# State-space layer of a decoder trunk: projections reordered and placed by tables, decay differences moved from VectorE to ScalarE, output product in two passes

## The chip, the cores and the metric

The kernel runs on one core of a Trainium2 chip. The metric is the device time of one execution in microseconds (us). Five engines matter. TensorE (PE) does the matrix products and ScalarE (ACT) the activations. VectorE (DVE) and GpSimd (POOL) do elementwise work, and SyncE (SP) issues the transfers (DMA).

## The reference

512 tokens of width 1024 go through two layers, each followed by a gated MLP with a short convolution, and a final normalisation. The first layer mixes by pooling and windowed attention; the second is the state-space layer that the change rewrites:

```python
def ssd_mixer(h, w_in, conv_w, conv_b, dt_bias, A_log, D_skip, norm_w, w_out):
    proj = h @ w_in
    z, xbc, dt = jnp.split(proj, [SSM_D_INNER, SSM_D_INNER + SSM_CONV_DIM], axis=-1)
    xbc = jax.nn.silu(causal_dwconv(xbc, conv_w, conv_b))
    xs, Bm, Cm = jnp.split(xbc, ...)
    dt = jax.nn.softplus(dt + dt_bias)
    A = -jnp.exp(A_log)
    y = ssd_scan(xs, dt, A, Bm, Cm) + D_skip[:, None] * xs
    y = y.reshape(B, S, SSM_D_INNER) * jax.nn.silu(z)
    y = rms_norm(y, norm_w, SSM_NORM_EPS)
    return y @ w_out

# in ssd_scan, by chunks of 128 tokens, with a = dt * A and its running sum a_cs in a chunk:
    Lmat = jnp.exp(jnp.where(tril, a_cs[..., :, None] - a_cs[..., None, :], -jnp.inf))
    CB = jnp.einsum("bclgn,bcsgn->bgcls", Cc, Bc)
    y_diag = jnp.einsum("bgcls,bgrcls,bcsgrp->bclgrp", CB, Lmat, X)
    states = jnp.einsum("bclgn,bgrcl,bclgrp->bcgrpn", Bc, decay, X)
    # state of chunk c+1 = state of chunk c * chunk_decay + states[c]
    y_off = jnp.einsum("bclgn,cbgrpn,bgrcl->bclgrp", Cc, prev, jnp.exp(a_cs))
    return y_diag + y_off
```

There are 8 groups of 4 heads with 64 features each, a state of 128, and 4 chunks.

## The kernel before

Everything lies with features on the 128 partitions and the 512 tokens along the free axis. A product of the trunk is a weight tile of eight 128x128 blocks against eight activation tiles. Weights and activations are split in a high and a low part, so each block costs three matmuls of 128x512 (L151 high by high, L152 high by the activation's low part, L153 the weight's low part): 24 matmuls for a product. `load_split` brings a weight tile: a DMA into `w`, ACT makes the high part `wh` (L143), DVE the low part `wl` (L144); each has three buffers.

The program is mixer, MLP, `ssm`, MLP. In the mixer the order of PE is written out by hand; `ssm` and the MLPs lie outside that block, and there a scheduler orders the instructions of every engine, with the place in the program as the priority. Whatever order comes out, each engine then works through its own list strictly in order.

In `ssm` the step sizes and decays come first (L663 to L665 are the running sums; L672 writes them to the scratch tensor `scr`). Then each group does six products: gates z (two), x (two), B and C. x, B and C go through a convolution (L286, L290, L292) and a Silu (L698 for z, L690 for the others). B and x are transposed (L710, L719), and B against C gives `cb` (L728, L730). For each of four chunks a DMA spreads four rows of `scr` over the partitions into `R` (L740). Then:

```python
for r in range(4):
    V.tensor_scalar(L[:, r, :], R[:, r, :], acs[:, h0 + r : h0 + r + 1], 0.0,
                    op0=ALU.subtract, op1=ALU.min)          # L743, DVE
A.activation(L[:], L[:], AF.Exp)                            # L745
```

L746 multiplies by `cb`, L749 and L750 make the state's factor (ACT, POOL). L754 and L757 are the output matmuls into `yp`, L760 the state product (from `XD`, which POOL makes in L723), and L763 or L766 the state update. L772 and L774 add the skip term and the gate into `yv`, and `stat.add` gathers squares (L224 ACT, L225 POOL).

After the eight groups `split_scaled` splits the 16 tiles `yv` (L204 on ACT for the high part, L205 on DVE for the low part), and eight output products of 48 matmuls with `wso` follow, one after the other.

The helpers `Line` (a list of product steps with side work placed at numbered steps) and `ahead` (issues a weight load one product early) are there before, used by the mixer.

## Time and profile before

| | us |
|---|---|
| median of the runs | 1314.21 |
| the other two runs | 1313.87 and 7378.31 |
| the profiled execution | 1316.71 |
| its span in the trace | 1314.9 |

The mean granted clock of TensorE is 0.992 in the profiled execution. Between 510 us (the feature steps of `ssm`, L628) and 943 us (the sums of the second MLP, L232) lies the part that the change rewrites. An engine's busy time is the sum of its instructions; rows of a timeline give the start, the length and, in brackets, the idle time just before and what ended it.

### The profile page before, as it was taken

The numbers are of one execution on the slowest core, as the hardware profiler recorded it, in microseconds if no ns is written. First come the engines' busy times: TensorE is split into PE (matmuls) and PEld (weight loads), VectorE is DVE, ScalarE is ACT, GpSimd is POOL, SyncE is SP. The second block draws the span as 40 slices with busy tenths as digits, with TensorE's granted clock in tenths as the row PEclk, the third lists the DMA queues.
The fourth block names the chain that finished last, engine by engine and source line by source line (L and its number), as shares of the span: only waits on it lengthen the run. The fifth ranks groups of instructions, "written<-read, shape, count | busy, mean of one in ns | idle before, by whom it ended". The sixth has DMA issues, their size and how long they took to land.

```text
span 1314.9 us, 16324 instructions
## 1 busy us (share of the span) xinstructions
PE 1288.2 (98%) x6280; PEld 1055.2 (80%) x6280; DVE 868.6 (66%) x1342; ACT 596.5 (45%) x829; POOL 182.4 (14%) x168
## 2 busy tenths in 40 slices
PE   8999999999999999999999999899999999999997
PEld 5766888888888887888888888688888888888887
DVE  7664577467547763788888888864587467547753
ACT  6254554234324443665556655633354234334442
POOL 4661300000000012022222122212000000000011
PEclk9999999999999999999999999999999999999999
DMA  7412232332333323333333333223322332332221
GB/s 239 129 48 65 81 96 87 106 96 92 98 101 96 98 82 112 95 116 118 107 97 108 101 112 103 79 75 98 97 96 84 108 96 90 89 111 96 80 81 65
DMA packets 41870, 129.16 MB, mean 98 GB/s; under 512 B 5120, under 2 KB 7424, under 8 KB 41792
## 3 DMA queue, kind: packets, MB, share of 16 engines
q1 hardware_dynamic: 41152, 126.81, 30.9%
q0 software_dynamic: 640, 1.31, 0.3%
q8 instruction: 49, 0.80, 0.3%
q14 instruction: 29, 0.24, 0.1%
HBM read 124.10 MB, written 2.16 MB: 96 GB/s over the span
## 4 chain that ended last, share of the span: by engine, by line
PE 92%; DVE 3%; DMA 1%; ACT 1%; issue 1%; POOL 0%; SPq 0%; DVEq 0%; ACTq 0%
PE mm L153 29%; PE mm L152 29%; PE mm L151 29%; PE yp L754 1%; PE ax L760 1%; PE yp L757 1%; DMA w<-wdn 1%; PE ax L719 1%; PE yp L508 1%; PE ax L728 0%; DMA x<-xT 0%; PE ax L248 0%; PE ax L232 0%; ACT c L530 0%; PE ax L554 0%
## 5 line engine op out<-in xcount | busy, mean ns | idle before, releaser
L152 PE MATMUL mm<-a,wh 128*128 128x512 f32 x1232 | 483.7, 393 | 5.6 <-DVE a L205 5.5
L151 PE MATMUL mm<-a,wh 128*128 128x512 f32 x1232 | 485.4, 394 | 0.8 <-ACT wh L814 0.7
L153 PE MATMUL mm<-a,wl 128*128 128x512 f32 x1232 | 485.3, 394 | 0.5 <-DVE wl L817 0.4
L143 ACT ACTIVATE wh<-w 128x1024 fp32r<-128x1024 f32 (+1 forms) x208 | 215.9, 1041 | 421.1 <-PE mm L152 375.4
L144 DVE TENSOR_TENSOR wl<-w,wh 128x1024 fp32r<-128x1024 f32 (+1 forms) x208 | 262.3, 1263 | 82.9 <-ACT wh L143 81.3
L152 PEld LDWEIGHTS mm<-a,wh 128*128 128x128 f32 x1232 | 232.7, 189 | 55.5 <-DVE a L205 7.2
L151 PEld LDWEIGHTS mm<-a,wh 128*128 128x128 f32 x1232 | 232.5, 189 | 51.8 <-issue 1.6
L153 PEld LDWEIGHTS mm<-a,wl 128*128 128x128 f32 x1232 | 232.5, 189 | 51.3 <-issue 2.0
L225 POOL TENSOR_TENSOR sacc<-sacc,sq 128x512 f32<-128x512 f32 (+1 forms) x55 | 78.6, 1429 | 874.9 <-ACT sq L224 873.6
L286 DVE TENSOR_TENSOR p<-mm,rb 128x512 f32<-128x512 f32 x120 | 82.3, 688 | 91.7 <-PE mm L153 84.4
L292 DVE SCALAR_TENSOR_TENSOR acc<-p,par,acc 128x511 f32<-128x511 f32 (+1 forms) x176 | 130.5, 747 | 3.7 <-ACT acc L290 0.9
L283 DVE TENSOR_TENSOR x<-mm,x 128x512 f32<-128x512 f32 x56 | 38.0, 689 | 107.6 <-PE mm L153 107.5
L152 PE MATMUL mm<-c,wh 128*128 128x512 f32 x240 | 93.5, 391 | 0.0
L153 PE MATMUL mm<-c,wl 128*128 128x512 f32 x240 | 92.7, 390 | 0.0
L151 PE MATMUL mm<-c,wh 128*128 128x512 f32 x240 | 92.3, 391 | 0.3 <-ACT c L204 0.3
L292 DVE SCALAR_TENSOR_TENSOR c<-p,par,c 128x511 f32<-128x511 f32 (+2 forms) x96 | 76.1, 794 | 1.7 <-ACT c L290 0.6
L290 ACT ACTIVATE acc<-p,par 128x512 f32<-128x512 f32 x88 | 70.7, 808 | 5.0 <-DVE p L286 4.2
L151 PE MATMUL mm<-b,wh 128*128 128x512 f32 x176 | 70.2, 402 | 0.7 <-ACT b L561 0.7
L152 PE MATMUL mm<-b,wh 128*128 128x512 f32 x176 | 68.4, 391 | 0.6 <-DVE b L562 0.6
L153 PE MATMUL mm<-b,wl 128*128 128x512 f32 x176 | 68.0, 390 | 0.0
L750 POOL TENSOR_TENSOR R<-R,c 128x512 f32<-128x512 f32 x24 | 37.6, 1582 | 195.0 <-ACT R L749 135.0
L373 ACT ACTIVATE acc<-acc 128x512 f32<-128x512 f32 x44 | 27.8, 631 | 78.6 <-DVE acc L292 78.6
(207 smaller groups left out, 1329.9 us busy)
## 6 DMA issues: line engine op xcount, KB each, us to landing
w<-wup SPq DMA_DIRECT2D x88, 512.0 KB, 3.5
w<-wsi SPq DMA_DIRECT2D x48, 512.0 KB, 3.5
w<-wdn SPq DMA_DIRECT2D x32, 448.0 KB, 3.3
w<-wdn SPq DMA_DIRECT2D x16, 512.0 KB, 3.7
R<-scr SPq DMA_DIRECT2D x32, 256.0 KB, 3.6
w<-wso SPq DMA_DIRECT2D x16, 512.0 KB, 3.6
w<-wmi SPq DMA_DIRECT2D x8, 512.0 KB, 4.6
w<-wmo SPq DMA_DIRECT2D x8, 512.0 KB, 3.6
```

Source lines behind the costliest of these rows:

```text
L143: A.activation(h[:, :kt, :cols], w[:, :kt, :cols], AF.Copy)
L144: V.tensor_tensor(out=l[:, :kt, :cols], in0=w[:, :kt, :cols], in1=h[:, :kt, :cols].bitcast(F32), op=ALU.subtract)
L151: PE.matmul(ps, lhsT=h[:, k, :], rhs=rh[k][:, ts], start=first and k == 0, stop=False)
L152: PE.matmul(ps, lhsT=h[:, k, :], rhs=rl[k][:, ts], start=False, stop=False)
L153: PE.matmul(ps, lhsT=l[:, k, :], rhs=rh[k][:, ts], start=False, stop=last and k == kt - 1)
L225: self.lanes[lane].tensor_tensor(out=acc[:, :w], in0=acc[:, :w], in1=sq[:, :w], op=ALU.add)
L283: V.tensor_tensor(out=x[:, n, :], in0=ps[:], in1=x[:, n, :], op=ALU.add)
L286: V.tensor_tensor(out=out, in0=ps, in1=rb[:], op=ALU.mult)
L290: A.activation(dst, src, AF.Identity, scale=pc(taps[-1]), bias=pc(b))
L292: V.scalar_tensor_tensor(out=dst[:, s:], in0=src[:, : T - s], scalar=pc(taps[-1 - s]), in1=dst[:, s:], op0=ALU.mult, op1=ALU.add)
L373: A.activation(g[:], g[:], AF.Silu)
L750: G.tensor_tensor(out=R[:], in0=R[:], in1=Ct[:, cs].unsqueeze(1).to_broadcast([P, 4, P]), op=ALU.mult)
```

## The change

`ssm` is written in another order. The products of a group come as B, C, x, x, z, z instead of z, z, x, x, B, C. All weight loads, those of `wso` too, go through `ahead`. The side work of a group hangs at numbered steps of a `Line` (one step is three matmuls) by three tables, one for the first group, one for the last and one for the others; the scheduler still has the last word, as `ssm` stays outside the hand-ordered block. The running sums (`decays`) come at step 46, and the outputs of a group in two halves, chunks 0 and 1, then 2 and 3. Chunk 3's `R` is asked for when the first half has been issued. The three state products stand together. The differences of the running sums are made by ACT (Relu of the negated difference, L761, followed by Exp with scale -1, L762) instead of DVE. The output product does the first eight feature tiles of n = 0 to 3, then their second eight, then n = 4 to 7 whole; the splits of `yv` are spread over the last group and the first output products. Two small ACT instructions that floated to the front of the kernel (an Exp and a Sqrt) are held in program order. Numbers of lines shift: L143 becomes L148, L151 to L153 become L156 to L158, L204 is L209, L224 is L229, L290 is L295, L690 and L698 are L718 and L708, L719 is L744 and L710 is L723 (transposes), L749 is L766, L754 and L757 are L795 and L798, L760 is L774.

```diff
+FIRST_AT = (24, 31, 53, 43, 50, 61, 72, 86)
+GROUP_AT = (26, 33, 36, 42, 50, 60, 70, 82)
+LAST_AT = (22, 28, 31, 40, 48, 64, 70, 80)
...
     def ssm(cur, nxt):
-        rb, rt = cur.stat.finish(D, EPS)
-
...
+        line = Line()
+        tiles = [t for g in range(GROUPS) for t in (32 + g, 40 + g, 16 + 2 * g, 17 + 2 * g, 2 * g, 2 * g + 1)]
+        halves = [(n, h) for h in range(2) for n in range(4)] + [(n, h) for n in range(4, KD) for h in range(2)]
+        take = ahead([lambda t=t: load_split(io["wsi"][t]) for t in tiles]
+                     + [lambda n=n, h=h: load_split(io["wso"][n, :, 8 * h : 8 * h + 8, :]) for n, h in halves])
...
-            for c in range(NB):
...
-                for r in range(4):
-                    V.tensor_scalar(L[:, r, :], R[:, r, :], acs[:, h0 + r : h0 + r + 1], 0.0,
-                                    op0=ALU.subtract, op1=ALU.min)
-                A.activation(L[:], L[:], AF.Exp)
...
+        def weights_of(g, c):
+
+            cs, h0 = slice(c * P, (c + 1) * P), c * NH + 4 * g
+            R = groups[g]["R", c] = tp.tile([P, 4, P], F32, tag="R", name=nm("R"), bufs=3)
+            nc.sync.dma_start(R[:], scr[h0 : h0 + 4, :].partition_broadcast(P))
+            L = groups[g]["L", c] = tp.tile([P, 4, P], F32, tag="L", name=nm("L"), bufs=3)
+
+            for r in range(4):
+                A.activation(L[:, r, :], R[:, r, :], AF.Relu, scale=-1.0, bias=acs[:, h0 + r : h0 + r + 1])
+            A.activation(L[:], L[:], AF.Exp, scale=-1.0)
+            V.tensor_tensor(out=L[:], in0=L[:], in1=groups[g]["cb"][:, cs].unsqueeze(1).to_broadcast([P, 4, P]),
+                            op=ALU.mult)
+            if c:
+                A.activation(R[:], R[:], AF.Exp)
+                G.tensor_tensor(out=R[:], in0=R[:], in1=groups[g]["C"][:, cs].unsqueeze(1).to_broadcast([P, 4, P]),
+                                op=ALU.mult)
+
+        def states(g):
+            u, psts = groups[g], []
+            for c in range(NB - 1):
+                pst = (mm() if c == 2 else aux())[:, :256].rearrange("p (r d) -> p r d", r=4)
+                PE.matmul(pst, lhsT=u["Bk"][:, c * P : (c + 1) * P], rhs=u["XD"][:, c], start=True, stop=True)
+                psts.append(pst)
...
+        def outputs(g, half):
+            u = groups[g]
+            if half == 0:
+                u["Y"] = yps2()
+            for c in (2 * half, 2 * half + 1):
...
+            if half == 0:
+                weights_of(g, 3)
+                return
...
+            if g == GROUPS - 1:
+                split_y(range(12, 16), ct)
...
+        line.at(17, lambda: hurry(step_sizes))
+        line.at(46, lambda: hurry(decays))
+        for g in range(GROUPS):
...
+                line.product(take, KD, cur.hs, cur.ls, done)
+            b = 6 * KD * g
+            tb, ti, tw, tx0, tx1, ts, to0, to1 = LAST_AT if g == GROUPS - 1 else GROUP_AT if g else FIRST_AT
+            line.at(b + tb, lambda g=g: turn_b(g))
+            line.at(b + ti, lambda g=g: inner(g))
+            for c in range(NB - 1):
+                line.at(b + tw + 4 * c, lambda g=g, c=c: weights_of(g, c))
...
+            line.at(b + ts, lambda g=g: states(g))
+            line.at(b + to0, lambda g=g: outputs(g, 0))
+            line.at(b + to1, lambda g=g: outputs(g, 1))
+
+
+        end = 6 * KD * GROUPS
+        for pos, fs, home in ((end - 6, range(4), ct), (end, range(4, 8), at), (end + 16, range(8, 12), at)):
+            line.at(pos, lambda fs=fs, home=home: split_y(fs, home))
...
+        for n, h in halves:
+            line.steps += [(lambda n=n, f=f: out_step(n, f)) for f in range(8 * h, 8 * h + 8)]
+        line.at(end + 51, sums2)
+        line.at(end + 60, spread2)
+        line.at(end + 64, lambda: out_done(3))
+        line.run()
```

Three places of the engines' lists show the move. The first is PE at the first group's running sums (`ax` from `sd`), in the kernel before, in the middle of a product `mm`:

```order
L151 MATMUL mm_4226<-a_3590,wh_4221 128x512
L152 MATMUL mm_4226<-a_3591,wh_4221 128x512
L663 MATMUL ax_3854<-sd,con 128x128
L664 MATMUL ax_3854<-sd,con 128x128
L665 MATMUL ax_3854<-con,sd 128x128
L153 MATMUL mm_4226<-a_3590,wl_4222 128x512
```

The same in the changed kernel, where the sums stand 14 rows further on in PE's list:

```order
L156 MATMUL mm_4120<-a_3746,wh_4071 128x512
L157 MATMUL mm_4120<-a_3747,wh_4071 128x512
L695 MATMUL ax_4101<-sd,con 128x128
L696 MATMUL ax_4101<-sd,con 128x128
L697 MATMUL ax_4101<-con,sd 128x128
L744 MATMUL ax_4133<-con,c_4027 128x128 x4
L158 MATMUL mm_4120<-a_3746,wl_4072 128x512
L156 MATMUL mm_4120<-a_3785,wh_4071 128x512
```

In the changed kernel the first outputs of that group come after two more products, split by the transposes of the next group's B (L723):

```order
L157 MATMUL mm_4318<-a_3514,wh_4257 128x512
L158 MATMUL mm_4318<-a_3513,wl_4258 128x512
L795 MATMUL yp_4294<-L_4152,X_4085 64x128 x4
L156 MATMUL mm_4318<-a_3551,wh_4257 128x512
L157 MATMUL mm_4318<-a_3552,wh_4257 128x512
L158 MATMUL mm_4318<-a_3551,wl_4258 128x512
L723 MATMUL ax_4331<-con,c_4168 128x128 x4
L156 MATMUL mm_4318<-a_3590,wh_4257 128x512
L157 MATMUL mm_4318<-a_3591,wh_4257 128x512
L158 MATMUL mm_4318<-a_3590,wl_4258 128x512
L795 MATMUL yp_4294<-L_4188,X_4085 64x128 x4
L798 MATMUL yp_4294<-R_4186,S_4226 64x128 x4
```

The sums moved back by those rows, and the outputs of the first group fall into three pieces; in the other groups but the last into two. Before, three of the eight groups had three pieces and five had two.

The second place is ACT at the change from the last group to the output product, before. `L` and `R` are the weights of chunks 0 to 2, `wh` weight tiles, `a` the high parts of `yv` (L204), `sq` squares, `c` from `p` a convolution's start:

```order
L745 ACT_TABLE_LOAD
L745 ACTIVATE L_6588<-L_6588 128x512
L745 ACTIVATE L_6605<-L_6605 128x512
L749 ACTIVATE R_6603<-R_6603 128x512
L143 ACTIVATE wh_6750<-w_6749 128x1024
L290 ACTIVATE c_6439<-p_6471,par 128x512
L745 ACTIVATE L_6631<-L_6631 128x512
L749 ACTIVATE R_6629<-R_6629 128x512
L143 ACTIVATE wh_6780<-w_6779 128x1024
L204 ACTIVATE a_6684<-b_3865,par 128x512
L224 ACTIVATE sq_6324<-b_3868 128x512
L224 ACTIVATE sq_6329<-b_3868 128x512
```

The same place in the changed kernel, where `c` from `b` are the high parts of the first four tiles of `yv`:

```order
L761 ACTIVATE L_6558<-R_6556,sd 128x128 x4
L762 ACTIVATE L_6558<-L_6558 128x512
L766 ACTIVATE R_6556<-R_6556 128x512
L718 ACT_TABLE_LOAD
L718 ACTIVATE c_6483<-c_6483 128x512
L229 ACTIVATE sq_6522<-b_3806 128x512
L148 ACTIVATE wh_6656<-w_6655 128x1024
L209 ACTIVATE c_6593<-b_3803,par 128x512
L229 ACTIVATE sq_6527<-b_3806 128x512
L209 ACTIVATE a_6638<-b_3804,par 128x512
L708 ACTIVATE c_6570<-c_6570 128x512
L209 ACTIVATE c_6597<-b_3803,par 128x512
```

The four differences of each chunk are new on ACT, and the splits alternate between two sets of tiles, with the last group's gate (L708) among them.

The third place is PE there, in the kernel before: `mm` with 6748 and 6837 are the output products n = 0 and n = 1, which alternate.

```order
L151 MATMUL mm_6748<-a_6684,wh_6750 128x512
L152 MATMUL mm_6748<-a_6685,wh_6750 128x512
L153 MATMUL mm_6748<-a_6684,wl_6751 128x512
L151 MATMUL mm_6748<-a_6688,wh_6750 128x512
L152 MATMUL mm_6748<-a_6689,wh_6750 128x512
L153 MATMUL mm_6748<-a_6688,wl_6751 128x512
L151 MATMUL mm_6748<-a_6692,wh_6750 128x512
L151 MATMUL mm_6837<-a_6684,wh_6839 128x512
L152 MATMUL mm_6837<-a_6685,wh_6839 128x512
```

And in the changed kernel, where 6654 and 6685 are n = 0 and n = 1:

```order
L158 MATMUL mm_6654<-c_6601,wl_6583 128x512
L157 MATMUL mm_6685<-c_6602,wh_6656 128x512
L158 MATMUL mm_6685<-c_6601,wl_6657 128x512
L795 MATMUL yp_6775<-L_6473,X_6573 64x128 x2
L795 MATMUL yp_6775<-L_6535,X_6573 64x128 x3
L156 MATMUL mm_6654<-c_6605,wh_6582 128x512
L156 MATMUL mm_6685<-c_6605,wh_6656 128x512
L795 MATMUL yp_6775<-L_6535,X_6573 64x128
L774 MATMUL ax_6716<-XD_6636,c_6420 128x256
L774 MATMUL ax_6718<-XD_6636,c_6420 128x256
L774 MATMUL mm_6720<-XD_6636,c_6420 128x256
L157 MATMUL mm_6654<-c_6606,wh_6582 128x512
```

The output products alternate as before, and the last group's first outputs (L795) and its state products (L774) stand among them; its outputs fall into five pieces.

## Rows read from the trace of the kernel before

**Rows 1.** the page's part 1: busy time and share of the span, instructions.

```profile
PE 1288.2 (98%) x6280; PEld 1055.2 (80%) x6280; DVE 868.6 (66%) x1342; ACT 596.5 (45%) x829; POOL 182.4 (14%) x168
```

**Rows 2.** stretch, length, busy PE, PEld, DVE, ACT, POOL (counts), clock, DMA share, GB/s.

```profile
530.00:845.00 315.00, 312.33 (x1716) 256.32 (x1715) 262.57 (x483) 191.18 (x249) 68.02 (x41) 0.99 0.34 106
560.00:812.00 252.00, 252.00 (x1407) 207.25 (x1406) 210.67 (x380) 148.74 (x191) 63.82 (x38) 1.00 0.34 107
831.50:834.30 2.80, 0.16 (x1) 0.00 (x0) 2.80 (x3) 2.79 (x4) 1.02 (x1) 1.00 0.00 0
834.30:838.10 3.80, 3.78 (x10) 3.02 (x11) 3.80 (x6) 3.09 (x5) 0.00 (x0) 0.55 0.40 138
845.00:880.00 35.00, 33.69 (x194) 26.49 (x192) 23.33 (x37) 14.35 (x19) 10.01 (x6) 1.00 0.15 46
```

**Rows 3.** PE's waits from 560 to 950 us: total, times, longest.

```profile
PE mm L152 <- DVE a L205: 2.7, 1, 2.7
PE ax L760 <- POOL XD L723: 0.9, 1, 0.9
PE mm L151 <- ACT c L204: 0.3, 1, 0.3
```

**Rows 4.** the chain that ended last, from 812 to 836 us: start, length.

```profile
814.44 4.13 DMA R<-scr
...
818.59 0.88 DVE L L743 x4
...
822.50 0.96 ACT wh L143
...
829.94 1.45 DVE c L292
...
833.53 0.75 DVE a L205
```

**Rows 5.** PE's timeline at one batch of outputs.

```profile
812.28 0.39 PE L152 MATMUL mm<-a,wh 128*128 128x512 f32 x1
812.51 0.39 PE L153 MATMUL mm<-a,wl 128*128 128x512 f32 x1
812.83 1.09 PE L754 MATMUL yp<-L,X 128*64 128x128 f32 x16
...
814.63 0.61 PE L757 MATMUL yp<-R,S 128*64 128x128 f32 x8
815.16 0.70 PE L760 MATMUL ax<-XD,c 128*128 128x256 f32 x2
```

**Rows 6.** ACT by line and shape, 530 to 950 us: busy us, mean ns, idle before.

```profile
L143 ACT ACTIVATE wh<-w 128x1024 fp32r<-128x1024 f32 x64 | 67.1, 1052 | 76.1 <-PE mm L152 66.7 <-issue 8.7 <-ACT a L204 0.8
...
L690 ACT ACT_TABLE_LOAD x16 | 20.5, 1283 | 2.5 <-DVE c L292 2.2
...
L745 ACT ACTIVATE L<-L 128x512 f32<-128x512 f32 x32 | 19.5, 628 | 9.0 <-DVE L L743 7.0 <-PE mm L152 1.7
...
L204 ACT ACTIVATE a<-b,par 128x512 fp32r<-128x512 f32 x8 | 5.4, 707 | 0.0
```

**Rows 7.** ACT by line and shape, 0 to 160 us.

```profile
L530 ACT ACTIVATE c<-c,st 128x128 f32<-128x128 f32 x8 | 3.1, 388 | 0.0
...
L461 ACT ACTIVATE vt<-ax,rt 128x128 f32<-128x128 f32 x4 | 1.1, 368 | 0.4 <-PE ax L459 0.4
```

**Rows 8.** DVE by line and shape, 530 to 950 us.

```profile
L743 DVE TENSOR_SCALAR L<-R,sd 128x128 f32<-128x128 f32 x128 | 28.2, 283 | 9.8 <-DMA R<-scr 8.1 <-PE yp L754 1.6
```

**Rows 9.** timeline of all engines at the first group's running sums.

```profile
550.64 0.38 PE L663 MATMUL ax<-sd,con 128*128 128x128 f32 x2
...
553.84 0.33 SPq L672 DMA_DIRECT2D scr<-sd  x1
...
555.43 1.28 SPq L740 DMA_DIRECT2D R<-scr  x3
...
559.08 0.87 DVE L743 TENSOR_SCALAR L<-R,sd 128x128 f32<-128x128 f32 x4 [0.77 <-DMA R<-scr]
```

More of the change, by code (lines that the diff above doesn't have):

```diff
@@ L692, in ssm @@
[L692 to L706 removed]
+        v, groups, early = {}, [{} for _ in range(GROUPS)], []
@@ new lines, in v3, with hurry, sums, spread @@
+        def v3(a):
+            return a.rearrange("p (c h) -> p c h", h=NH)
+        def hurry(fn):
+            with tc.high_priority(offset=HURRY):
+                fn()
+        def sums():
+            with tc.high_priority(offset=HURRY):
+                v["rt"] = cur.stat.sums(D, EPS)
+        def spread():
+            with tc.high_priority(offset=HURRY):
+                v["rb"] = cur.stat.spread(v["rt"])
+            for fn in early:
+                fn()
+        def steps_of_features():
+            dfm = mm()
+            for k in range(KD):
+                q = slice(k % 4 * NH, k % 4 * NH + NH)
+                PE.matmul(dfm[q, :], lhsT=wd[:, k, :], rhs=x[:, k, :], start=k < 4, stop=k >= 4)
+            v["dfs"] = t2("p", 3)
+            A.activation(v["dfs"][:], dfm[:], AF.Copy)
@@ new lines, in gate, with convolved @@
+        def gate(g, i, ps):
+            z = groups[g]["z", i] = ct()
+            scaled(ps[:], v["rb"], z[:])
+            A.activation(z[:], z[:], AF.Silu)
+        def convolved(g, name, c, ps):
+            if "rb" not in v:
+                early.append(lambda: convolved(g, name, c, ps))
+                return
+            dst = groups[g][name] = ct()
+            p = t2("p", 3)
+            scaled(ps[:], v["rb"], p[:])
+            conv(p[:], dst[:], tuple(C_SW + 32 * i + c for i in range(4)), C_SB + c)
+            A.activation(dst[:], dst[:], AF.Silu)
@@ L723, in ssm, with inner @@
[L723 to L724 removed]
+        def inner(g):
             pcb = aux()
@@ new lines, in states @@
+        def states(g):
[4 more added lines that the diff above has]
+                psts.append(pst)
+            for c, pst in enumerate(psts):
+                h0 = c * NH + 4 * g
+                new = u["S", c + 1] = tp.tile([P, 4, 64], F32, tag="S", name=nm("S"), bufs=3)
+                if c == 0:
+                    V.tensor_copy(new[:], pst)
+                else:
+                    for r in range(4):
+                        V.scalar_tensor_tensor(out=new[:, r, :], in0=u["S", c][:, r, :],
+                                               scalar=dbc[:, h0 + r : h0 + r + 1], in1=pst[:, r, :],
+                                               op0=ALU.mult, op1=ALU.add)
@@ L758, in ssm @@
[L758 to L769 removed]
+                        PE.matmul(yr[r], lhsT=u["S", c][:, r, :], rhs=u["R", c][:, r, :], start=False, stop=True)
@@ new lines, in ssm, with out_step @@
+        end = 6 * KD * GROUPS
+        for pos, fs, home in ((end - 6, range(4), ct), (end, range(4, 8), at), (end + 16, range(8, 12), at)):
+            line.at(pos, lambda fs=fs, home=home: split_y(fs, home))
+        acc = {}
+        def out_step(n, f):
+            if f == 0:
+                acc[n] = mm()
+            if f % 8 == 0:
+                acc[n, "ws"] = take()
+            gemm(acc[n][:], [w[:, f % 8 : f % 8 + 1, :] for w in acc[n, "ws"]], 1, [kh[f]], [kl[f]],
+                 first=f == 0, last=f == 15)
+            if f == 15 and n >= 4:
+                out_done(n)
```

213 lines of the change are left out of this document (85 added, 128 removed).

## The prediction

> **What bounds the kernel now.** The page's busy times come first. PE is busy for 1288.2 us of a span of 1314.9 [rows 1], so nothing that leaves PE's own work alone can gain more than some 26 us in the whole kernel. The question is where PE stands idle inside the rewritten part. The table of stretches answers it: from 530 to 845 us PE is busy for 312.33 of 315.00, and from 560 to 812 us for 252.00 of 252.00 [rows 2]. In the steady groups there is nothing to win but PE's own work. The idle time lies at the end, where the last group meets the output product.
>
> PE's list of waits for the whole of 560 to 950 us has three entries: 2.7 us for DVE's split of `yv` (L205), 0.9 for POOL's `XD`, 0.3 for ACT's split [rows 3]. After the longest the clock is low as well: in 3.80 us from 834.3 the granted clock is 0.55, while it is 1.00 before and after [rows 2]. That costs 3.8 x 0.45 = 1.7 us more. From 845 to 880 us, with the wait of 0.9 in it, the clock stays at 1.00, so a wait of that size did not lower it.
>
> The chain of waits tells how the 2.7 us arise: an `R` lands 4.13 us after its issue, DVE makes the four differences, ACT the Exp, a weight tile and DVE convolution steps follow, and the split comes last, at 833.53 [rows 4]. DVE is 83% busy from 530 to 845 us (262.57 of 315) [rows 2], and at the end one queue carries differences, convolutions and splits.
>
> **What the change takes away.** The 128 differences leave DVE: 28.2 us of busy time [rows 8], of which all lies beside PE's work except in the tail. With the early splits the tail of before need not come back in its old form. I count all of it as gone: 2.7 idle, 1.7 slow clock, 0.9 and 0.3 for the two small waits, **5.6 us** together. Other waits take their place, counted below.
>
> **What it adds on ACT.** 128 Relus of 128x128 with a pointer operand. The lower bound is the L461 row, four in 1.1 us, so 0.28 each and 36 us in all; the upper one is L530, 388 ns each and 50 us [rows 7]. I take the lower, since there too four stand in a row. ACT goes from 191 us of 315 [rows 2] to 227 (72%; 77% at the upper bound), DVE from 83% to 74%. Both still have a quarter of the time free, so in the six middle groups I cost the move at **nothing**; what covers it are the products of 24 matmuls at 0.23 us [rows 5], 5.5 us each. The tightest point is chunk 3. `L` has three buffers, so its Relus wait until PE has read the first half of the outputs. Then come four Relus (1.1), a table load (1.28) and two Exps of 0.63 [rows 6, 7], 3.6 us, and POOL's product. The halves stand 12 steps of three matmuls apart, 8.2 us. A weight tile (1.05) that stands between still fits. The number of table loads in the groups stays: one pair of Exp and Silu sets for each block of chunks.
>
> At the tail the cover is thinner, and at the start of the layer too:
>
> **The start.** The running sums come 14 rows later on PE, 14 x 0.23 = 3.2 us, at about 553.8 instead of 550.64. From the sums to the landed `R` it took 559.08 - 550.64 = 8.4 us before [rows 9], so `R` lands at about 562.3. The first weights are then ready after Relu 1.1, table load 1.28, Exp 0.63 and DVE's product by `cb` (about 0.7, an estimate: a 128x512 pass such as those of ACT): 566.0, if ACT is free; 570.2, if a Silu between two loads (1.28 + 0.63 + 1.28) and a weight tile (1.05) stand ahead [rows 6]. PE reaches the first outputs after 55 matmuls, transposes and state products, 14.6 us after the sums, at 568.4. So the first set waits between 0 and 1.8 us. The second set comes 1.8 us of PE's work later (six matmuls and the transposes) and needs another four Relus, two Exps and POOL's product, so it can wait about as much again. Bounds 0 and 4; I take the middle, **+2.0**. All later work queues behind PE there, so a wait counts in full.
>
> **The tail.** Between the last gate product on PE (24 x 0.23 = 5.5, and transposes 0.4, together 5.9 us) ACT's list holds Relus 1.1, two Exps 1.3, a table load 1.28, Silu 0.63, a square 0.63, a weight tile 1.05 and the first high part of `yv` 0.71: 6.7 us. That is 0.8 behind, if both begin together. From the first high part to the fourth ACT then has nine pieces: a square, the gate, six high parts and a weight tile, 0.63 + 0.63 + 6 x 0.71 + 1.05 = 6.6 us [rows 6], and PE has 18 matmuls (4.1), seven outputs (0.8) and the borders of two fragments (0.4): 5.3. Another 1.3 behind, **+2.1** in all. The lower bound is 0 (ACT may begin earlier than PE by what it is free), the upper twice that, 4.2, with `XD` late as before. Later splits have a product or more in hand.
>
> **Fragments.** A batch of outputs costs PE something at its borders. The first set starts 0.32 after the last matmul where 0.23 is the step (812.28 to 812.51), and four sets take 1.80, 0.45 each, but the last 0.53 [rows 5]: 0.2 us a batch. The lists give 19 batches before and 20 after (the first group three, the last five, six with two), so **+0.2**. The three state products together, the third in a product's buffer, are the same matmuls; the new order of tiles, B and C first, only changes which side work waits for which product.
>
> **The queues.** SP's list has the same transfers. Weight loads come one product ahead, with three buffers as before; `R` of chunk 3 is asked for when the first half of the outputs has been issued and lands 4.13 us later [rows 4], inside the 8.2. Queued behind a waiting `R` on SP is the next weight load, which has a product of 5.5 us in hand. The two ACT instructions held in order move at most a table load of 1.28 us either way [rows 6], beside an ACT that is 45% busy [rows 1]: 0.
>
> **The sum.** 1316.71 - 5.6 + 2.0 + 2.1 + 0.2 = 1315.4 for an execution such as the profiled one. That one was 2.5 us above the median of 1314.21, so the forecast is 1312.9, rounded to **1313**, 0.1% faster. A measurement of this kernel tells about 2% from no change, 26.3 us: below 1287.9 or above 1340.5.
>
> **Rivals.**
> 1. All new waits are covered. The splits of the first twelve tiles are early in the program, and DVE has 28 us less. Then 1316.71 - 5.6 + 0.2 - 2.5 = 1308.8. Against it: ACT's list is fixed, and the sums above leave it behind PE.
> 2. The new waits are long enough to lower the clock, as the one of 2.7 did. Each then costs 1.7 more: 1314.7 with one, 1316.4 with both; with both waits at their upper bounds (+4.1), 1320.5. For: the wait at the start is up to 4. Against: 0.9 did not lower it [rows 2, 3], and both waits fall into several pieces.
> 3. ACT becomes the bound in every group, and the kernel ends slower. ACT works in order. A Relu whose `R` has not landed, or whose `L` buffer PE still reads, holds up the weight tiles and Silus behind it; these come late, so PE comes late to the next half, and so on. Each group then pays its wait w at the chunk 3 point, and 1.7 for the clock when w is long. From 1313 to 1340.5 it takes 27.5 us, 3.4 in each of eight groups: it decides from w of 1.7 us. At w = 1 without the clock it is 1321. For: the differences needed no more than 283 ns each on an engine that had them near its product by `cb` [rows 8], and ACT has up to 388 [rows 7]. Against: 72 to 77% busy, and 8.2 us between the halves for 3.6 us of work plus POOL's.
> 4. The tables don't set the order, since the scheduler does, and the tail keeps its old stall in another place: 2.7 and 1.7 stay, 1316.7 - 1.2 + 2.0 + 0.2 - 2.5 = 1315.2. For: the two output products still alternate in the list. Against: DVE's differences are gone from the tail in any case.
>
> On rival 3 the Trainium skill ("ScalarE: Activation LUTs", section "Rules for kernel authors") has a rule that speaks against this change: relu, max, min and add belong on VectorE, not on ScalarE. By that rule the move is a loss of the difference of the two engines; the rows agree on the sign (28.2 us against 36 to 50), but the loss lies beside PE's work as long as ACT has room, so it enters the sum only through rival 3.
>
> **How the numbers follow.** The forecast's case (1311 to 1316, with rival 4 in it at 0.1) has 0.5, rival 1 (1306 to 1311) 0.22, rival 2 (1316 to 1321) 0.16, rival 3 0.1, of which 0.03 above 1340.5; 0.02 is left for a larger gain. The range from 1306 to 1319 leaves out rival 3, the upper third of rival 2 and the rest, under 0.2. Faster by over 2% gets 0.01: it would need all of PE's idle time and more. Slower by over 2% gets 0.03, the rest 0.96.
>
> **What would show it.** L761 should be 128 pieces of 280 to 390 ns; DVE's busy time in the layer should fall by some 28 us and ACT's rise by 36 to 50. PE should have no idle time between 580 and 810 us, a wait on the first group's outputs near 568 us with `R` landing at about 562, and small waits on ACT's or DVE's split near 830 us, with the granted clock at 1.00 through them. A clock below that, in a stretch behind such a wait, is rival 2. PE idle in each middle group before the second half of the outputs is rival 3. The forecast is wrong if the two waits are absent, or if a queue that I counted as free (SP's with the early loads above all) delays a weight tile.

## The result and the profile after

The changed kernel takes 1316.67 us in the median of 20 runs (1315.1 to 1321.35), beside 1313.97 for the kernel before (20 runs, 1312.38 to 1316.32, and one far outside at 7378.31). The ratio is 1.0024, with a 95% interval from 1.0018 to 1.0030. That lies inside the forecast's range and within 2%, but on the other side: 0.24% slower, where 0.1% faster was forecast. The profiled execution took 1315.61 us, its span is 1313.8. It is one of the faster ones, 1.1 us under the median, while the profiled execution before was 2.5 above the median of its three; so what the change does is read in the part that it rewrites, and the medians tell what it comes to.

The page's part 1 answers to [rows 1]:

```profile
PE 1283.8 (98%) x6280; PEld 1051.8 (80%) x6280; DVE 850.6 (65%) x1214; ACT 629.7 (48%) x954; POOL 177.9 (14%) x168
```

ACT has 33.2 us more, a little under the forecast's 36 to 50, though the 128 Relus take 41.2 us by themselves. DVE has 18.0 less, not 28 (the last section shows where it went). PE's first 2214 and last 2023 instructions are of the same shapes in both kernels, so the time between can be compared. The rows at both points, before and then after, are in PE's timelines:

```profile
510.68 1.92 PE L628 MATMUL mm<-x,wd 128*32 128x512 f32 x14
888.04 0.48 PE L151 MATMUL mm<-c,wh 128*128 128x512 f32 x1
510.48 0.39 PE L156 MATMUL mm<-a,wh 128*128 128x512 f32 x1
889.62 0.39 PE L156 MATMUL mm<-a,wh 128*128 128x512 f32 x1
```

The stretch takes 377.36 us before and 379.14 after, 1.8 more. Behind it, where the work is the same, the profiled execution before has 426.9 us left and the other one 424.2. What PE waits for from 500 to 960 us (line, what it waited for: total, times, longest) answers to [rows 3]:

```profile
PE ax L774 <- POOL XD L750: 2.9, 2, 2.2
PE yp L795 <- DVE L L763: 1.7, 2, 1.2
PE mm L157 <- DVE c L210: 1.5, 1, 1.5
PE ax L731 <- ACT c L718: 0.8, 1, 0.8
PE mm L156 <- ACT c L209: 0.7, 1, 0.7
PE yp L798 <- POOL R L767: 0.5, 1, 0.5
```

Their sum is 8.0 us (2.9 is 2.25 and 0.61), where [rows 3] had 3.9. PE's timeline tells where they lie. Four of its eight idle times, two of the start and then two of the tail:

```profile
573.35 0.66 PE L795 MATMUL yp<-L,X 128*64 128x128 f32 x8 [1.23 <-DVE L L763]
...
605.37 0.92 PE L774 MATMUL ax<-XD,c 128*128 128x256 f32 x3 [2.25 <-POOL XD L750]
...
838.77 0.73 PE L156 MATMUL mm<-c,wh 128*128 128x512 f32 x2 [0.66 <-ACT c L209]
841.39 0.50 PE L157 MATMUL mm<-c,wh 128*128 128x512 f32 x1 [1.51 <-DVE c L210]
```

Before 606 us lie 5.2 us (0.45 at 569.44, 1.23, 0.47 at 574.48, 0.84 at 581.64, 2.25). Between 606 and 830 us there is nothing. The wait at 581.64 (`ax`, B against C, L731) and the one at 605.37 (the state products) belong to the second group. The tail has 2.8 us (0.66, 1.51 and 0.61 at 847.77). The loss is at the start, in the stretch where the first group ends and the second begins. The table of stretches, columns as in [rows 2], shows it on ACT:

```profile
560.00:812.00 252.00, 246.75 (x1378) 202.06 (x1377) 195.11 (x280) 180.24 (x299) 55.72 (x37) 1.00 0.34 106
565.00:605.00 40.00, 35.12 (x200) 27.61 (x198) 29.97 (x36) 34.94 (x58) 10.30 (x7) 1.00 0.29 91
605.00:645.00 40.00, 39.63 (x224) 32.66 (x225) 32.38 (x46) 28.19 (x47) 9.21 (x7) 1.00 0.36 116
645.00:685.00 40.00, 40.00 (x227) 32.96 (x226) 31.02 (x45) 27.98 (x46) 8.90 (x6) 1.00 0.36 106
```

From 565 to 605 us ACT is busy for 34.94 of 40 us, 87%; in each later group for 28, 70%. The same 40 us of the kernel before, the first stretch of that table there:

```profile
565.00:605.00 40.00, 40.00 (x229) 33.09 (x228) 34.68 (x63) 25.13 (x32) 12.65 (x7) 1.00 0.36 106
```

So ACT got 9.8 us more into that stretch, not the 4.5 that it got into the later ones (28.0 against some 23.5 before). ACT's timeline there, from the first Relu on, shows what it does:

```profile
561.47 1.28 ACT L761 ACTIVATE L<-R,sd 128x128 f32<-128x128 f32 x4 [3.80 <-DMA R<-scr]
563.49 1.28 ACT L761 ACTIVATE L<-R,sd 128x128 f32<-128x128 f32 x4 [0.74 <-DMA R<-scr]
564.79 1.28 ACT L718 ACT_TABLE_LOAD   x1
566.08 0.63 ACT L718 ACTIVATE c<-c 128x512 f32<-128x512 f32 x1
566.73 1.28 ACT L762 ACT_TABLE_LOAD   x1
568.03 0.63 ACT L762 ACTIVATE L<-L 128x512 f32<-128x512 f32 x1
...
579.67 1.28 ACT L718 ACT_TABLE_LOAD   x1
580.96 0.63 ACT L718 ACTIVATE c<-c 128x512 f32<-128x512 f32 x1
582.89 0.63 ACT L718 ACTIVATE c<-c 128x512 f32<-128x512 f32 x1 [1.29 <-DVE c L297]
...
590.15 1.28 ACT L718 ACT_TABLE_LOAD   x1 [0.69 <-DVE c L297]
591.45 0.63 ACT L718 ACTIVATE c<-c 128x512 f32<-128x512 f32 x1
592.10 1.28 ACT L762 ACT_TABLE_LOAD   x1
593.39 0.63 ACT L762 ACTIVATE L<-L 128x512 f32<-128x512 f32 x1
```

First ACT stands still for 3.80 us at the head of its list, for the first `R`. Then the first group's Exps and the second group's Silus alternate, and each change costs a load of 1.28 us: seven from 564.79 to 598.25. The order before has seven between 553 and 605 us, two of them ahead of 560. There `R` had landed 2.4 us earlier, at 559.08 [rows 9], and the Relus, 1.28 us for four, were on DVE.

How that becomes the wait of 2.25 us at 605.37 is read from DVE's timeline, and from POOL's for the last row:

```profile
594.05 0.69 DVE L763 TENSOR_TENSOR L<-L,c 128x512 f32<-128x512 f32 x1 [2.66 <-ACT L L762]
594.66 1.79 DVE L806 TENSOR_TENSOR b<-b,c 128x512 f32<-128x512 f32 x1
...
596.98 0.68 DVE L806 TENSOR_TENSOR b<-b,c 128x512 f32<-128x512 f32 x1
...
598.18 1.98 DVE L149 TENSOR_TENSOR wl<-w,wh 128x1024 fp32r<-128x1024 f32 x1
...
601.68 1.48 DVE L149 TENSOR_TENSOR wl<-w,wh 128x1024 fp32r<-128x1024 f32 x1 [0.32 <-ACT wh L148]
603.08 0.68 DVE L746 TENSOR_TENSOR X<-ax,sd 128x512 f32<-128x512 f32 x1
603.84 1.47 POOL L750 TENSOR_TENSOR XD<-X,sd 128x768 f32<-128x768 f32 x1 [1.76 <-DVE X L746]
```

DVE is idle for 2.66 us, until ACT's Exp after its last two table loads. From then on it is busy but for 0.32 us, and its list is late: the second `X` starts at 603.08. POOL makes `XD` from it from 603.84 in 1.47 us, and PE starts 0.06 us later. ACT's list had waited for DVE before that (1.29 us at 582.89, 0.69 at 590.15): the two lists wait for each other in turn.

### The profile page after: what moved, and what is told of

Read it like the earlier page. It is cut to its first block, busy times and chain, and to the rows that moved or that the text cites. A ratio compares the mean times of both kernels' runs of the same rounds, so it can differ in the third digit from the quotient of the medians.

```text
span 1313.8 us, 16320 instructions
## 1 busy us (share of the span) xinstructions
PE 1283.8 (98%) x6280; PEld 1051.8 (80%) x6280; DVE 850.6 (65%) x1214; ACT 629.7 (48%) x954; POOL 177.9 (14%) x168
## 4 chain that ended last, share of the span: by engine, by line
PE 89%; ACT 3%; DVE 3%; issue 2%; DMA 1%; POOL 1%; DVEq 0%; ACTq 0%; POOLq 0%
PE mm L156 28%; PE mm L157 28%; PE mm L158 27%; PE yp L795 1%; DVE c L297 1%; DMA w<-wdn 1%; PE yp L798 1%; PE yp L513 1%; DVE wl L149 1%; ACT L L761 1%; ACT wh L148 1%; PE ax L774 1%; PE ax L253 0%; PE ax L237 0%; PE ax L731 0%
## 5 line engine op out<-in xcount | busy, mean ns | idle before, releaser
L156 PE MATMUL mm<-a,wh 128*128 128x512 f32 x1232 | 487.4, 396 | 0.3 <-ACT wh L899 0.3
L158 PE MATMUL mm<-a,wl 128*128 128x512 f32 x1232 | 481.0, 390 | 1.1 <-DVE wl L902 1.1
L148 ACT ACTIVATE wh<-w 128x1024 fp32r<-128x1024 f32 (+1 forms) x208 | 216.0, 1042 | 413.1 <-PE mm L157 373.3
L149 DVE TENSOR_TENSOR wl<-w,wh 128x1024 fp32r<-128x1024 f32 (+1 forms) x208 | 259.1, 1249 | 80.7 <-ACT wh L148 79.3
L156 PEld LDWEIGHTS mm<-a,wh 128*128 128x128 f32 x1232 | 231.8, 188 | 53.1 <-issue 5.4
L158 PEld LDWEIGHTS mm<-a,wl 128*128 128x128 f32 x1232 | 231.8, 188 | 50.4 <-DVE wl L902 2.0
L156 PE MATMUL mm<-c,wh 128*128 128x512 f32 x240 | 92.1, 390 | 0.7 <-ACT c L209 0.7
L158 PE MATMUL mm<-c,wl 128*128 128x512 f32 x240 | 92.6, 389 | 0.0
L295 ACT ACTIVATE acc<-p,par 128x512 f32<-128x512 f32 x88 | 70.7, 808 | 4.8 <-DVE p L291 4.2
L156 PE MATMUL mm<-b,wh 128*128 128x512 f32 x176 | 70.1, 402 | 0.7 <-ACT b L566 0.7
L158 PE MATMUL mm<-b,wl 128*128 128x512 f32 x176 | 68.0, 390 | 0.0
```

What stands on the lines that cost most here:

```text
L148: A.activation(h[:, :kt, :cols], w[:, :kt, :cols], AF.Copy)
L149: V.tensor_tensor(out=l[:, :kt, :cols], in0=w[:, :kt, :cols], in1=h[:, :kt, :cols].bitcast(F32), op=ALU.subtract)
L156: PE.matmul(ps, lhsT=h[:, k, :], rhs=rh[k][:, ts], start=first and k == 0, stop=False)
L158: PE.matmul(ps, lhsT=l[:, k, :], rhs=rh[k][:, ts], start=False, stop=last and k == kt - 1)
L295: A.activation(dst, src, AF.Identity, scale=pc(taps[-1]), bias=pc(b))
```

## The experiments

All were timed in five rounds beside the kernel before. "Idle" is the sum of PE's waits from 500 to 960 us in the profiled execution of each: 3.9 us before, 8.0 after.

**1 to 3. The two halves of the change apart.** First the changed kernel with the differences back on DVE:

```diff
-                A.activation(L[:, r, :], R[:, r, :], AF.Relu, scale=-1.0, bias=acs[:, h0 + r : h0 + r + 1])
-            A.activation(L[:], L[:], AF.Exp, scale=-1.0)
+                V.tensor_scalar(L[:, r, :], R[:, r, :], acs[:, h0 + r : h0 + r + 1], 0.0,
+                                op0=ALU.subtract, op1=ALU.min)
+            A.activation(L[:], L[:], AF.Exp)
```

> The changed kernel with the differences back on DVE (subtract and min, Exp with scale 1); order, tables and the two passes stay. Theory A (the Relus in ACT's in-order list make the start and the tail late): PE's idle time in the layer falls from 8.0 us to under 4, the start and second group from 5.2 to under 2, and the time to about 1312 us. Theory B (it is the places in the tables, above all the late running sums): idle time within 1.5 us of the changed kernel's, 1316 to 1317 us, since the engine that makes the differences waits for the same transfers.

Measured: 1315.82 us, ratio 1.0015 [1.0005, 1.0025], idle 6.1. The next one is the kernel before with the opposite edit alone:

> The kernel before with the differences moved to ACT, nothing else. Theory A: ACT is late in the tail and at the start of the layer, new waits of 2 to 5 us, 1315 to 1319 us. Theory B: the freed DVE shortens the tail's wait of 2.7 us, nothing else moves, 1310 to 1314.

Measured: 1321.37 us, ratio 1.0053 [1.0040, 1.0066], idle 8.2. The waits of the first (order new, DVE), then the first four of the second (order old, ACT):

```profile
PE mm L157 <- DVE c L210: 3.4, 3, 2.1
PE ax L775 <- POOL XD L750: 2.5, 6, 0.7
PE yp L796 <- DVE X L746: 0.2, 1, 0.2
```

```profile
PE mm L152 <- DVE a L205: 3.0, 2, 2.6
PE mm L153 <- DVE wl L144: 1.6, 2, 1.2
PE ax L728 <- DVE X L721: 1.1, 5, 0.2
PE ax L710 <- ACT c L690: 1.1, 5, 0.2
```

With the kernels before and after these make a table of two by two: old order 1314.0 with DVE and 1321.4 with ACT, new order 1315.8 with DVE and 1316.7 with ACT. In the old order the move costs 7 us, in the new one 1; on DVE the new order costs 2. The two parts are not added up, and each edit also lets the scheduler make another list: with the differences on DVE in the new order, ACT has 48 table loads from 530 to 950 us instead of 36. With DVE the start of the new order is nearly free (0.7), and five middle groups wait 0.35 to 0.41 us each for `XD`, behind DVE; with ACT the middle is free and the start is not.

The start of the first kernel (new order, DVE) says more than that. Its running sums stand as late as in the changed kernel (553.73 us), and its list has the same seven table loads from 564 to 605 us. What it lacks there are the Relus:

```profile
565.00:605.00 40.00, 39.17 (x219) 31.31 (x218) 38.92 (x73) 28.49 (x38) 11.06 (x7) 1.00 0.34 110
```

ACT is busy for 28.49 of the 40 us, not 34.94, and one wait of 0.68 is left. So the late sums and the loads don't make the waits without the Relus. Nor do the Relus in the old order: the second kernel has one wait of 0.53 us at the start, with ACT busy for 32.51 of these 40 us. Its idle time is 4.3 us above that of before, and 7 are measured. Some 2.7 of them are no idle time and no low clock: outside both, PE's own steps take 374.4 us of the stretch, beside 371.7 before. Why was not tried.

Third, the differences on POOL (`G.tensor_scalar`, as in the diff above):

> The changed kernel with the differences on POOL. If the lists of ACT and DVE are what is short at both ends of the layer: the start's and the tail's idle time both fall, 8.0 us to under 4, 1311 to 1313 us. Rival: POOL's own passes are so long that its products by C and XD come late, and DVE's passes beside them get longer: new waits on POOL in every group, 1318 us or more.

Measured: 1325.81 us, ratio 1.0096 [1.0082, 1.0109]. A piece takes 935 ns on POOL (mean of 128), and `XD`, made on POOL too, keeps PE waiting for 5.8 us in the second group.

**4. The running sums earlier**, by the table:

```diff
-        line.at(46, lambda: hurry(decays))
+        line.at(40, lambda: hurry(decays))
```

> The changed kernel with the running sums at step 40 instead of 46, 4.1 us of PE's work earlier. Theory B: the waits of the first group's outputs (0.45, 1.23 and 0.47 us near 570 us) go, and what follows from them with them (0.84 near 582 and 2.25 near 605): about 1312 us. Theory A: R lands 4 us earlier, so the first waits shrink by up to 2.1 us, but the backlog on ACT in the second group stays, with the wait for XD near 605: 1314.5 to 1316.

Measured: 1315.79 us, ratio 1.0013 [1.0004, 1.0021], idle 5.7. The sums did not come earlier (555.54 us against 553.90, of which 1.0 lies ahead of 510 us): the scheduler only put other work behind them. The waits between 569 and 582 us went, and one of 2.56 us for `XD` came at 565.05. A position in the table is a wish, not a place.

**5. The first `R` early.** The first group's `R` comes from a second scratch tensor, written at the layer's start:

```diff
+        nc.sync.dma_start(scr0[:], ident)
...
+            nc.sync.dma_start(R[:], (scr0 if g == 0 else scr)[h0 : h0 + 4, :].partition_broadcast(P))
```

> The changed kernel, but the first group's R comes from a scratch tensor that is written when the layer begins (the constant identity), so the first group's differences use other data and its outputs are not the reference's; work and transfers stay, R no longer waits for the running sums. Theory H (at the start ACT's list stands at Relus whose R has not landed, 3.8 us, and all that is behind them comes late: the Silu of B and C, the splits of weights, X): PE's idle time near 570 to 605 us goes from 5.2 to under 1 us, the tail keeps its 2.8, about 1312 to 1313.5 us. Rival (the first two groups carry too much side work whenever R lands): 3 us or more stay, 1315 or more.

Measured: 1315.64 us, ratio 1.0020 [1.0011, 1.0029], idle 7.1. PE's idle times at the start are then these, in its timeline:

```profile
580.14 1.16 PE L733 MATMUL ax<-c,c 128*128 128x128 f32 x8 [1.71 <-ACT c L720]
598.96 0.50 PE L158 MATMUL mm<-a,wl 128*128 128x512 f32 x1 [0.27 <-DVE wl L149]
604.11 1.13 PE L776 MATMUL ax<-XD,c 128*128 128x256 f32 x4 [2.35 <-POOL XD L752]
```

The waits of the outputs near 570 us, 2.15 us together, are gone. The second group's are not: 1.71 us at B against C, where it had 0.84, and 2.35 for `XD`. ACT still stands at its first Relu for 3.94 us, since the Relus read the sums as well, but until 555.06 and not until 561.47. The late `R` explains the first outputs and not the second group.

**6 to 8. No table switches in the second group.** A plain Copy takes the place of that group's Silus, in the changed kernel:

```diff
-            A.activation(z[:], z[:], AF.Silu)
+            A.activation(z[:], z[:], AF.Copy if g == 1 else AF.Silu)
...
-            A.activation(dst[:], dst[:], AF.Silu)
+            A.activation(dst[:], dst[:], AF.Copy if g == 1 else AF.Silu)
```

> The changed kernel with a plain copy in place of the Silu of the second group (B, C, x and the gates), so that group needs no switch between the Silu and Exp tables; its values are not the reference's, all else stays. If the table loads in ACT's list are what holds up that group: the waits near 582 and 605 us (0.8 and 2.2) go, those near 570 and 574 shrink by what a load less brings, 5.2 us to under 2.5, 1313 to 1314.5 us. If it is the Relus and the late R alone: 4 us or more stay, 1316 or more.

Measured: 1311.59 us, ratio 0.9983 [0.9974, 0.9992], below both kernels. The waits of PE, then its stretch of 565 to 605 us:

```profile
PE mm L157 <- DVE c L210: 1.5, 1, 1.5
PE ax L774 <- POOL XD L750: 0.7, 1, 0.7
PE mm L156 <- ACT c L209: 0.7, 1, 0.7
```

```profile
565.00:605.00 40.00, 39.26 (x221) 31.71 (x220) 35.06 (x44) 26.87 (x54) 11.32 (x7) 1.00 0.37 120
```

One table load is left between 564 and 605 us, ACT has 8 us less, and 4.5 of the 5.2 us at the start are gone. DVE's list shows why, at the places that were shown above:

```profile
589.24 0.69 DVE L763 TENSOR_TENSOR L<-L,c 128x512 f32<-128x512 f32 x1
598.71 0.68 DVE L746 TENSOR_TENSOR X<-ax,sd 128x512 f32<-128x512 f32 x1
```

From the product by `cb` to the second `X` it takes 9.47 us, no less than the 9.03 of the changed kernel. But it begins 4.8 us earlier, without the wait of 2.66 for ACT's Exp. The measured gain over the changed kernel is 5.1 us. Whether the Copies make any order faster was asked of the kernel before, with the same edit:

> The kernel before, with a plain Copy in the place of the Silu of the second group (B, C, x and the gates), so that the values of that group are not the reference's; it is the same edit as in the run no_switch, made on the old order. Theory (the switches of ACT's tables cost the changed kernel its 5.2 us at the start only because the late sums leave ACT behind PE there): the old order has seven table loads between 553 and 605 us too, but only 0.9 us of idle time of PE in the layer away from the tail, so the edit gains little here: 1312.5 to 1314, ratio 0.999 to 1.0003, and the tail's wait of 2.7 stays. Rival (the Copy makes the kernel shorter by itself, through the values that PE multiplies or through a higher clock, whatever the order): 1309 to 1311, the same 4 to 5 us as in the changed kernel.

Measured: 1314.33 us beside 1313.84, ratio 0.9997 [0.9986, 1.0008]. ACT's busy time from 565 to 605 us falls from 25.13 to 21.05 us there too, and nothing comes of it. The switches cost nothing in the old order, and by experiment 1 next to nothing at the start of the new one without the Relus: what costs is the two together in the new order. Can an order with the reference's values have the gain? In the last one of this group the Silus of the second group's B and C are held next to each other, with a table of its own for that group:

```diff
+SECOND_AT = (34, 36, 39, 43, 50, 62, 71, 82)
...
+        def silu_bc(g):
+            for name in ("B", "C"):
+                dst = groups[g][name]
+                tc.keep_in_program_order(A.activation(dst[:], dst[:], AF.Silu))
```

> The changed kernel with the Silu of the second group's B and C held next to each other in program order, so that one table load serves both, and with a table of its own for the second group that asks for its outputs one step later (71) and its state products two steps later (62). All values are the reference's. Theory (table switches inside ACT's list, where the first two groups overlap): one or two of the seven table loads between 553 and 605 us go, 1.3 to 2.6 us of ACT's time, and of the 5.2 us of waits at the start 1.5 to 3 go: 1313.5 to 1315. Rival (what counts is the place of each piece in the list, not the number of loads): holding the two Silus back moves C's Silu ahead of a Relu or B's behind one, and the waits move to another instruction: 1316 to 1318, with 5 us of waits at the start as before.

Measured: 1317.32 us, ratio 1.0019 [1.0007, 1.0031], idle 6.3. From 564 to 605 us seven loads are left as before; the two Silus share one, another change came in. `XD` at the second group takes 2.6 us. The rival was right here.

**9 to 12. Other places for the pieces of the start.** First later outputs and state products, then the same with the early splits of experiment 13, then, on the first of these tables, later weights of the first group with their Relus held in program order:

```diff
-FIRST_AT = (24, 31, 53, 43, 50, 61, 72, 86)
-GROUP_AT = (26, 33, 36, 42, 50, 60, 70, 82)
+FIRST_AT = (24, 31, 53, 43, 50, 66, 79, 90)
+GROUP_AT = (26, 33, 36, 42, 50, 63, 70, 82)
```

> The changed kernel with the first group's states and outputs 5, 7 and 4 steps later on PE and the other groups' states 3 steps later. Theory B: the waits near 570, 582 and 605 us (5.2 us) go, the tail's 2.8 stay, about 1311 to 1312.5 us. Theory A: the backlog on ACT meets the second group as before, 2 us or more stay, 1314 or more.

> Both edits together, differences on ACT. Theory B: under 2 us of PE's idle time is left in the layer, 1309 to 1311 us, faster than the kernel before by 3 to 5 us. Theory A: 1312 or more.

> The changed kernel with the first group's weights asked for later and its Relus held in program order, states and outputs of the first group later, the other groups' states 3 steps later: in the order the Silu of the second group's B and C now stand ahead of most Relus. Theory H: idle time at the start under 1.5 us (only the first Relu still waits for R ahead of other work), tail 2.8 as before, 1312 to 1314 us. Rival: the wait turns up at another place, 3 us or more, 1316 or more.

Measured: 1317.46 (ratio 1.0031 [1.0021, 1.0041]), 1316.63 (1.0020 [1.0011, 1.0029]) and 1317.13 us (1.0027 [1.0015, 1.0038]), idle 6.0, 6.9 and 6.1. The waits of the start become one of 3.8 and 3.9 us in the first two, which in the second one's timeline of PE reads:

```profile
580.42 2.07 PE L731 MATMUL ax<-c,c 128*128 128x128 f32 x8 [3.86 <-ACT c L718]
```

The Silu of the second group's C stands behind Relus and switches. With the Relus behind it instead (the third kernel, whose table has 60 in the place of 53), the outputs wait 1.76 us for their weights and `XD` is 1.21 late. None of the three places helped. The second kernel with its differences on DVE:

> The same with the differences back on DVE. Theory B: within 1.5 us of the same kernel with the differences on ACT. Theory A: faster than that by 2 us or more. If DVE was what the change rightly relieved: slower by 2 us or more, with waits on DVE's split in the tail.

Measured: 1315.68 us, ratio 1.0017 [1.0007, 1.0026], idle 6.6, of it 1.6 in four middle groups.

**13 to 16. The tail.** In the changed kernel the first four splits three steps earlier, then the output product in one pass, with earlier places for the last group's work and the later splits:

```diff
-        for pos, fs, home in ((end - 6, range(4), ct), (end, range(4, 8), at), (end + 16, range(8, 12), at)):
+        for pos, fs, home in ((end - 9, range(4), ct), (end, range(4, 8), at), (end + 16, range(8, 12), at)):
```

```diff
-LAST_AT = (22, 28, 31, 40, 48, 64, 70, 80)
+LAST_AT = (22, 28, 31, 40, 48, 50, 52, 56)
...
-        halves = [(n, h) for h in range(2) for n in range(4)] + [(n, h) for n in range(4, KD) for h in range(2)]
+        halves = [(n, h) for n in range(KD) for h in range(2)]
...
-        for pos, fs, home in ((end - 6, range(4), ct), (end, range(4, 8), at), (end + 16, range(8, 12), at)):
+        for pos, fs, home in ((end - 6, range(4), ct), (end, range(4, 8), at), (end + 4, range(8, 12), at)):
```

> The changed kernel with the split of the first four tiles of yv nine steps before the output product instead of six. In the order ACT's first high part then stands ahead of two blocks of Relu and Exp, and DVE's low part ahead of the second output tile's weight. Theory B (places, not engines, make the waits): the tail's waits on the splits (0.66 and 1.51 us) go, the start's 5.2 us stay: about 1314 to 1315 us. Theory A (ACT and its Relus are short of time there): the waits only move to the next tiles, 1316 to 1317.

> The changed kernel with the output product done n by n, the last group's outputs and the later splits placed earlier to serve it (one pass). If the two passes are what removed the long wait of the kernel before (theory C): a wait of 2 us or more on a split comes back in the tail, at times with a low clock behind it, 1318 to 1321 us. If the early splits and the freed DVE removed it: the tail's idle time stays near 2.8 us, 1316 to 1317.

Measured: 1316.45 (ratio 1.0017 [1.0009, 1.0026]), with tail waits of 1.20 and 1.19 us in the place of 0.66 and 1.51; and 1318.99 us (1.0039 [1.0026, 1.0051]), with a tail of 3.4 and a granted clock of 0.50 from 845 to 850 us. The early splits only move the wait to the fourth tile. One pass with these places is some 2 us slower than the two passes in the new order, by two ratios whose intervals overlap; the places moved with it, so the passes have no price of their own. In the old order, for n = 0 to 3 and for n = 0 to 2:

```diff
+        acc = [mm() for n in range(4)]
+        for n in range(4):
+            ws = load_split(io["wso"][n, :, 0:8, :])
+            gemm(acc[n][:], ws, 8, kh, kl, last=False)
...
+            ps = acc[n] if n < 4 else mm()
+            for half in range(n < 4, 2):
```

> The kernel before with one part of the change alone: the output product in two passes for n = 0 to 3; differences on DVE, order of tiles, places and homes of the splits as before. In the order three output tiles now share each split of yv, nine matmuls or 2.0 us of PE's work for each, so the last group's outputs have a pass more time. If the two passes are the useful part of the change: the wait of 2.7 us on DVE's split and the low clock behind it go or shrink under 1 us, 1309.5 to 1312 us, faster than both. Rival: the first split of the batch is late on DVE's list in any case, the wait stays near 2.7 us and the time at 1313 to 1314.

> The kernel before with the output product in two passes for n = 0 to 2 alone. The wait of 1.9 us before n = 4 goes, since n = 3 whole (48 matmuls, 10.9 us) covers the second normalisation; the wait of 2.0 us on DVE's split and at times the low clock behind it stay: 1312 to 1313 us, 1 to 2 us faster than the kernel before. Rival: the last group's outputs then come late instead, 1314 or more.

Measured: 1314.07 us, ratio 0.9993 [0.9981, 1.0005], and 1315.89, 1.0016 [1.0007, 1.0024]. The wait for the split falls from 2.7 to 2.0 us in both, and a new one of 1.9 and 1.8 us stands behind the first pass. No kernel with the reference's values was shown to be faster than the one before.

## Why the forecast was near and its sign wrong

**What was right.** The five later middle groups are free, from 606 to 830 us. The sums stand at 553.90 us (forecast 553.8), the first `R` is there at 561.47 (562.3), four Relus take 1.26 to 1.28 us (1.1). ACT's busy time from 530 to 845 us is 225.1 (227). The old tail is gone, and its new waits are 2.8 us, above the 2.1 of the sum; they fall on ACT's high part and DVE's low part, as forecast, and 0.6 on `XD`, named at the upper bound. The granted clock is 1.00 through them in the profiled execution.

**The step that failed** is the one that was put at nothing: "in the six middle groups I cost the move at **nothing**". The second group is the first of these six, and PE waits 3.1 us in it: 0.84 at its B against C and 2.25 at its state products. The forecast's own sign, no idle time between 580 and 810 us, came out wrong at 581.64 and 605.37. "The start", **+2.0** with bounds 0 and 4, worked out the first group's outputs alone, and these came to 2.15 in three pieces; with the second group behind them the start has 5.2. The cover that was given for nothing was the mean busy share of 72% and "The number of table loads in the groups stays". The number did stay (33 for Exps and Silus from 530 to 950 us, 34 before). But in the second group the loads and the new Relus fall on a list of ACT that is already 3.80 us late, and the mean of 315 us hides a stretch with 87%.

What the runs showed in its place: the second group's waits need the Relus, the table switches and the new order together. Without the Relus 0.7 us is left at the start (experiment 1), without the switches 0.7 (experiment 6), in the old order 0.5 (experiment 2). An early `R` alone leaves 4.1 in that group (experiment 5). What it is in the new order that does it, the late sums or the places of the pieces, was not tried by itself: experiment 4 could not move the sums.

**The sum with measured terms.** Between the two points of the same shapes the kernel before has 3.9 us of waits and 1.7 of low clock, which went. The changed kernel has 8.0 of waits and no low clock. With these alone the sum is 377.4 - 3.9 - 1.7 + 8.0 = 379.8, against 379.14: PE's own steps, without waits and low clock, came out some 0.6 shorter. The forecast had -5.6 + 2.0 + 2.1 + 0.2 = -1.3 there and +1.8 was measured. Of the 3.1 between them the second group is 3.1, the first outputs are 0.15 and the tail is 0.7, less 0.8 on the 0.2 for fragments. No run shows that price of fragments: PE's own steps got shorter, not longer. In the medians the miss is larger, 2.7 us slower where 1.3 faster than the 1314.21 at hand was forecast. With one traced execution of each kernel the other 0.9 can't be placed. That the forecast for an execution such as the profiled one, 1315.4, lies 0.2 us from the profiled 1315.61 is luck: the 3.1 that it lacks in the stretch are nearly made good by the 2.7 that the same work behind it was faster in that execution.

**The rivals.** Rival 1 (all covered) is refuted by the waits. Rival 3 (every group waits because ACT is in order) has its mechanism in nearly every group. Besides the 3.80 us for the first `R`, the Relus of chunk 3 stand in six groups until PE has read `L`, by ACT's waits from 530 to 845 us:

```profile
ACT L L761 <- PE yp L795: 18.0, 6, 3.1
```

PE waits for nothing from 606 to 830 us all the same. Ahead of the tail only the first two groups pay, so the price is a few us. In the old order it reaches the middle groups as small waits (experiment 2). Rival 4 is half true: the scheduler, not the tables, decided where the sums stand (experiment 4), yet the tail's old wait did go. Rival 2 asked for a low clock behind each new wait. In the profiled execution there is none, in those of other kernels there is; next section. Its price with both waits, 1316.4, is near the median, but the stretch is 1.8 us longer without any. On the page's rule that relu belongs on VectorE (the Trainium skill, "ScalarE: Activation LUTs", section "Rules for kernel authors"): this case's new order agrees in sign by 0.9 us, with intervals of the two ratios that overlap, the old order by 7 us.

## What to carry to other kernels

Before work moves to an engine with a quarter of its time free, look for the stretch where that engine is late and changes tables most often, such as the overlap of the first two groups, and walk through its list instruction by instruction there; the mean over all groups does not show it. Follow the delay to the end of the stage: after the first output had waited, two more waits came from the same late list through DVE and POOL. When a delay has several conditions (here an order, an engine and the table switches), take each away by itself before one of them is called the cause. And compare traced executions between two points with the same work around them: outside of these the same work differed by 2.7 us.

## What the runs showed of the hardware that was not expected

- A low granted clock behind a wait is not certain. The 2.25 us at 605.37 left it at 1.00 in the changed kernel's profile; behind the same wait in experiment 13 (2.23 us) it was 0.73 from 605 to 610 us, and behind the 3.8 of experiment 9 it was 0.50, the lower of the two levels (1.2 GHz), from 580 to 585 us.
- DVE's busy time fell by 18 us, though 28.2 us of differences left it. Two of its operations took 8.8 of the other 10.2 us back: from 510 to 944 us the product by `cb` (L746, now L763) went from 682 to 781 ns, the last gate step (L774, now L806) from 683 to 955 ns. In experiment 2, with the Relus on ACT in the old order, both stay at 682 and 685. In the rows of DVE above L806 takes 1.79 us at 594.66 and 0.68 at 596.98. POOL's product `R` ran from 594.62 to 595.90, beside the first and not the second. Which accesses collide was not tried.
- In experiment 8 the records show a granted clock of 0.95 from 100 to 500 us, where the same stretch before has 1.00. PE's busy time in it is 397.68 us, against 397.60 before: that level in the records cost nothing.
